# A two-layer hybrid block on one core: the first mixer's latent products in two items and other banks, its filling pieces dealt out anew, its output projection begun two heads sooner

## The chip, the cores and the metric

The kernel runs as one launch on one core of a Trainium2 chip. The metric is the device time of one execution in microseconds (us); lower is better. The engines are named as in the profile: PE (TensorE, matrix products, with PEld for its weight loads), DVE (VectorE), ACT (ScalarE), POOL (GpSimd) and SP (SyncE, which here only issues transfers).

## The reference

Two layers run over 512 tokens of width 1024. Layer 0 mixes tokens with the "even mixer", layer 1 with another one, and a gated, convolved feed-forward network of width 2816 follows each. The change lies almost wholly in the even mixer:

```python
def even_mixer(h, positions, w_in, q_norm, w_uq, kv_norm, w_ukv, w_out):
    proj = h @ w_in
    q, k, v = ...                      # 12 heads of 64, three groups of four
    q, k = rope(q, positions), rope(k, positions)
    for window, dilation in ((128, 1), (512, 4), (2048, 16)):
        out, lse = dilated_window_attention(q[group], k[group], v[group], window, dilation)
    y_a = sum over the groups of softmax(lse) * out        # four heads of 64
    qm = rmsnorm(c_q, q_norm) @ w_uq   # 12 heads of 64 + 32, from a latent of 256
    kv = rmsnorm(c_kv, kv_norm) @ w_ukv  # 12 heads of 64 + 64, from a latent of 128
    y_b = causal_softmax_attention(q_full, k_full, v_m, 96 ** -0.5)
    return concatenate([y_a, y_b]) @ w_out    # 1024 -> 1024, added to x by the caller
```

## The kernel before

All values are fp32. A product is made of three matmuls of rounded halves (`mm3`: high by high, high by low, low by high). So each weight block is loaded as `wraw`, its high half `whi` is made by ACT (L220) and its low half `wlo` by DVE or POOL (L222). Two buffers of each kind serve all weights (`wchunk`). Activations are split in the same way into `xh` and `xl`.

The even mixer lays its attention out as 16 head steps: heads 0 to 5 and 8 to 13 are the latent ("MLA") heads in pairs `pr` 0 to 5, and heads 6, 7, 14 and 15 are the windowed ("dsw") heads, where one step serves one head of all three groups. A head's scores go to the PSUM banks `s`; DVE adds the mask and takes the extremum (L580), ACT takes the exponent and scales (L582, L584). PE then turns the weights around in the banks `t`, ACT and DVE split them into `pth` (L601, L954) and `ptl` (L602, L955), and PE applies them to the values in the banks `o`. While head k is turned and applied in `units`, the scores of head k+1 are made. There are two banks each of `s`, `t`, `o` and `proj`.

PE's order is fixed by the program (`InOrder`); the order on the other engines is chosen by a scheduler when the kernel is built. Between the steps of a head, PE gets *pieces* from a `Stream` of items: one piece is one product of three 512-column matmuls. `st.fill(n)` takes n pieces, `st.until(name)` takes as many as finish an item, and an item that is held (`holds`, with the head that frees it) blocks the stream. The items are: projections of q, k (`d{p}{g}{s}`) and v for the dsw heads, eight pieces each; the latent products `m{pr}` for a pair of MLA heads, six pieces; `y`, which splits the finished heads' outputs; and `o0` to `o7`, the output projection, one for each 128 rows of x. `F_M`, `F_D0` and `F_D1` say how many pieces a head takes after each score, after each turn and at its end, `F_V` how many around a value transpose.

Latent products use the banks `proj`: in `run_mla`, v (tile `vt`, L761), k (`knp`, L766), then two queries (`rt`, L775). The output projection runs over seven of the eight tiles of y; the eighth, from the last dsw pair, is added by `run_tail` after head 15, one product and one `residual` (L367) for each of the eight tiles of x. Then the feed-forward network's `norm` makes `xh` (L331) and `xl` (L332) of x.

Of the kernel before, what the change touches and what calls it, by code (L numbers as in the profile page):

```python
# [18 lines left out]
P = 128  # L19
# [32 lines left out]
F_V = 1, 2  # L52
F_M, F_D0, F_D1 = (1, 1, 2), (2, 1.5, 3), (2, 2, 4)
# [131 lines left out]
class Builder:  # L185
# [169 lines left out]
    def run_tail(self, src, kt, y, banks=("proj",)):  # L355

        def run(w):
            for m in range(KT):
                ps = self.psum(banks[m % len(banks)])
                self.gemm(ps, w, m * P, P, 0, {kt: y[kt][0]}, {kt: y[kt][1]}, [kt])  # L360
                self.residual(m, ps)
                yield

        return f"t{kt}", lambda: self.wchunk(src, D), run

# [143 lines left out]
    def ffn(self, pool, g, cw, cb, wg, wu, wd, tiles=KT):  # L509

        nc = self.nc
        pre = [self.wchunk(w[0], D) for w in (wg, wu)]
# [132 lines left out]
    def even_mixer(self, pool):  # L645
# [109 lines left out]

        def run_mla(pr):
            def run(w):
                vps = self.psum("proj")
                self.gemm(vps, w, 640, P, 0, klh, kll, [0])
                vt = pool.tile([P, T], F32, tag="tmp", name=self.nm("vt"), bufs=TMP)  # L760
                nc.vector.tensor_tensor(vt, vps, kr, op=ALU.mult)  # L761
                yield
                kps = self.psum("proj")
                self.gemm(kps, w, 512, P, 0, klh, kll, [0])
                knp = pool.tile([P, T], F32, tag="knp", name=self.nm("knp"), bufs=1)
                nc.vector.tensor_tensor(knp, kps, kr, op=ALU.mult)  # L766
                yield
                qs = []
                for e in range(2):
                    qps = self.psum("proj")  # L770
                    for i in range(2):
                        self.gemm(qps, w, e * P + i * 256, P, 256, qlh, qll, [i], i == 0, i == 1)
                        yield
                    t = pool.tile([P, T], F32, tag="tmp", name=self.nm("rt"), bufs=TMP)
                    nc.vector.tensor_tensor(t, qps, qt[e], op=ALU.mult)  # L775
                    qs.append(self.split(t, pool, **QK))
                    if e == 0:
                        v = self.token_split(pool, vt, "v", 3)
                yp = pool.tile([P, T], F32, tag="yp", name=self.nm("yp"), bufs=6)
                mla[pr] = qs, v, yp, knp  # L780

            return f"m{pr}", lambda: self.wchunk(a["wm0"][pr], 768), run

        def run_out(m):
            def run(w):
                yh, yl = {k: y[k][0] for k in range(7)}, {k: y[k][1] for k in range(7)}
                for ps in self.proj_pieces(w, yh, yl, range(7)):
                    yield
                self.residual(m, ps)

            return f"o{m}", lambda: self.wchunk(a["wo0"][m], 896), run

        def run_y():
            def run(w):
                for i in range(6):
# [7 lines left out]
        def y_split(kt, yp):  # L803
# [7 lines left out]
               for p in range(2)]  # L811
        m = [run_mla(pr) for pr in range(6)]
        st = Stream(dsw[0][:3] + m[:1] + dsw[0][3:4] + m[1:2] + dsw[0][4:6] + m[2:3] + dsw[0][6:]
                    + dsw[1][:2] + m[3:4] + dsw[1][2:4] + m[4:5] + dsw[1][4:6] + m[5:] + dsw[1][6:]
                    + [run_y()] + [run_out(m) for m in range(KT)])

        holds = {"d022": 5, "m3": 7, "d110": 7, "d122": 13, "y": 14}
# [47 lines left out]
        def mla_head(pr, e):  # L865
            hd = Head()
            hd.fill_s, hd.fill_u, hd.fill_g = F_M
# [31 lines left out]
            def finish():  # L899
                self.head_out(pool, hd.o, mla[pr][2], e)  # L900

# [826 lines left out]
```

## Time and profile before

| what | value |
|---|---|
| median of 3 runs | 1448.83 us (1447.15 to 1449.09) |
| the profiled execution's own time | 1443.72 us |
| its span, first to last instruction | 1441.7 us |
| mean granted TensorE clock in it | 0.993 |
| PE busy | 1380.4 us (96%) |
| DVE busy | 872.8 us (61%) |
| ACT busy | 696.3 us (48%) |

The even mixer takes the first 336 us of the span. An engine's row in a timeline may end with the idle time ahead of it and, behind an arrow, the instruction that ended it. A matmul's record lasts longer than its share of PE, since the next one starts before it ends; starts that follow each other give that share.

### The profile page before, as it was taken

To read this page: it belongs to the slowest core of one execution; us is meant where nothing else is said; L and a number is where in the kernel's file an instruction comes from. 1 tells how busy PE (TensorE), PEld (TensorE's weight loads), DVE (VectorE), ACT (ScalarE), POOL (GpSimd) and SP (SyncE) were. 2 spreads that over 40 slices of the span, in tenths; PEclk is the share of its full clock that TensorE was granted. 3 is DMA by queue.
4 is the path that set the end of the run, shared out by engine and by line. 5 is a ranking of instruction groups with operands and counts; after the bars stand their busy time and mean duration, and the time that the engine had idled before them with its cause. 6 is when DMAs were issued, how large, how long until landed. Compare 5 with 4: busy or idle time off the path is not lost.

```text
span 1441.7 us, 17940 instructions
## 1 busy us (share of the span) xinstructions
PE 1380.4 (96%) x6796; PEld 1139.2 (79%) x6796; DVE 872.8 (61%) x1393; ACT 696.3 (48%) x1151; POOL 413.1 (29%) x249
## 2 busy tenths in 40 slices
PE   7899899999999999999998998999999999999997
PEld 5677777787888888888887777787888888888886
DVE  7978778747555555212578997789555555552124
ACT  5578668735433333222366565787344333333322
POOL 2100000003655555444200000222025555554440
PEclk9999999999999999999999999999999999999998
DMA  5422122122233232333222111111222232333333
GB/s 169 121 58 61 56 70 68 42 68 88 88 103 98 93 102 88 104 96 93 90 84 68 59 45 61 47 57 48 75 92 95 100 102 88 103 99 93 97 95 99
DMA packets 40262, 121.19 MB, mean 84 GB/s; under 512 B 5233, under 2 KB 8305, under 8 KB 40177
## 3 DMA queue, kind: packets, MB, share of 16 engines
q1 hardware_dynamic: 38160, 117.92, 26.2%
q10 hardware_dynamic: 2016, 2.14, 0.5%
q8 instruction: 53, 0.87, 0.3%
q14 instruction: 33, 0.26, 0.1%
HBM read 114.80 MB, written 2.10 MB: 81 GB/s over the span
## 4 chain that ended last, share of the span: by engine, by line
PE 77%; DVE 14%; ACT 4%; issue 3%; DMA 1%; POOL 0%; SPq 0%; DVEq 0%; ACTq 0%; POOLq 0%
PE proj L113 48%; PE o L113 19%; PE z L113 5%; PE s L113 2%; DVE wlo L222 2%; PE t L116 2%; PE t L113 1%; ACT whi L220 1%; DVE cv L1153 1%; ACT s L582 1%; ACT s L584 1%; DVE xl L332 0%; DVE ptl L602 0%; DVE mh L266 0%; DVE xs L1393 0%
## 5 line engine op out<-in xcount | busy, mean ns | idle before, releaser
L222 POOL TENSOR_TENSOR wlo<-wraw,whi 128x1024 fp32r<-128x1024 f32 (+1 forms) x135 | 315.2, 2336 | 574.0 <-ACT whi L220 574.0
L220 ACT ACTIVATE whi<-wraw 128x1024 fp32r<-128x1024 f32 (+3 forms) x219 | 222.1, 1015 | 354.9 <-PE proj L113 322.7
L113 PE MATMUL proj<-xh,whi 128*128 128x512 f32 x844 | 341.8, 405 | 8.5 <-ACT xh L331 6.4
L113 PE MATMUL proj<-xh,wlo 128*128 128x512 f32 x844 | 332.7, 394 | 1.3 <-DVE wlo L388 1.1
L113 PE MATMUL proj<-xl,whi 128*128 128x512 f32 x844 | 332.9, 394 | 1.1 <-DVE xl L332 1.1
L113 PE MATMUL proj<-act,whi 128*128 128x512 f32 (+1 forms) x748 | 219.3, 377 | 0.0
L113 PEld LDWEIGHTS proj<-xh,whi 128*128 128x128 f32 x844 | 160.2, 190 | 40.8 <-ACT xh L331 8.6
L113 PEld LDWEIGHTS proj<-xh,wlo 128*128 128x128 f32 x844 | 160.0, 190 | 37.1 <-DVE wlo L388 1.5
L113 PEld LDWEIGHTS proj<-xl,whi 128*128 128x128 f32 x844 | 160.4, 190 | 31.0 <-DVE xl L332 3.0
L113 PEld LDWEIGHTS proj<-act,whi 128*128 128x128 f32 x748 | 137.7, 188 | 25.7
L113 PE MATMUL o<-xh,wlo 128*128 128x512 f32 x368 | 143.5, 390 | 0.0
L113 PE MATMUL o<-xh,whi 128*128 128x512 f32 x368 | 143.5, 390 | 0.0
L113 PE MATMUL o<-xl,whi 128*128 128x512 f32 x368 | 143.3, 389 | 0.0
L113 PE MATMUL proj<-act,wlo 128*128 128x512 f32 (+1 forms) x374 | 140.9, 377 | 0.0
L367 DVE TENSOR_TENSOR x<-x,proj 128x512 f32<-128x512 f32 x31 | 21.2, 685 | 171.6 <-PE proj L113 171.5
L525 DVE SCALAR_TENSOR_TENSOR cv<-gt,cols,cv 128x511 f32<-128x511 f32 x44 | 94.3, 2147 | 35.9 <-ACT cv L524 35.9
L222 DVE TENSOR_TENSOR wlo<-wraw,whi 128x1024 fp32r<-128x1024 f32 (+3 forms) x84 | 95.7, 1139 | 28.8 <-ACT whi L220 27.9
L528 ACT ACTIVATE sl<-cv 128x512 f32<-128x512 f32 x44 | 27.8, 631 | 127.3 <-DVE cv L526 127.3
L534 DVE TENSOR_TENSOR up<-sl,o 128x512 f32<-128x512 f32 x44 | 30.3, 688 | 91.9 <-POOL sl L529 91.9
L529 POOL TENSOR_TENSOR sl<-sl,rsr 128x512 f32<-128x512 f32 x44 | 57.8, 1313 | 94.3 <-ACT sl L528 94.3
L266 DVE TENSOR_TENSOR act<-up,act 128x512 fp32r<-128x512 f32 x44 | 63.2, 1437 | 29.3 <-ACT act L265 29.3
L113 PEld LDWEIGHTS proj<-act,wlo 128*128 128x128 f32 x374 | 70.4, 188 | 12.9
(305 smaller groups left out, 2126.7 us busy)
## 6 DMA issues: line engine op xcount, KB each, us to landing
wraw<-in_g SPq DMA_DIRECT2D x44, 512.0 KB, 3.4
wraw<-in_u SPq DMA_DIRECT2D x44, 512.0 KB, 3.3
wraw<-in_d SPq DMA_DIRECT2D x32, 448.0 KB, 3.3
wraw<-in_wqk SPq DMA_DIRECT2D x20, 512.0 KB, 3.6
wraw<-in_d SPq DMA_DIRECT2D x17, 512.0 KB, 3.5
wraw<-in_wx SPq DMA_DIRECT2D x12, 512.0 KB, 3.3
wraw<-in_wv SPq DMA_DIRECT2D x10, 512.0 KB, 3.5
wraw<-in_wz SPq DMA_DIRECT2D x8, 512.0 KB, 3.3
```

Of the source, the lines that this page charges most:

```text
L113: return self._put(self.b.nc.tensor.matmul(*args, **kw))
L116: return self._put(self.b.nc.tensor.transpose(*args))
L220: nc.scalar.activation(hi[:, :n], raw[:, :n], AF.Copy)
L222: (eng or self.lo).tensor_tensor(lo[:, :n], raw[:, :n], hi[:, :n].bitcast(F32), op=ALU.subtract)
L266: nc.vector.tensor_tensor(lo, src, hi.bitcast(F32), op=ALU.subtract)
L367: self.nc.vector.tensor_tensor(self.x[m], self.x[m], ps, op=ALU.add)
L525: nc.vector.scalar_tensor_tensor(c[:, 1:], gt[:, : T - 1], col_(1), c[:, 1:], op0=ALU.mult, op1=ALU.add)
L528: nc.scalar.activation(s, c, AF.Silu)
L529: nc.gpsimd.tensor_tensor(s, s, r, op=ALU.mult)
L534: nc.vector.tensor_tensor(u, s, pu, op=ALU.mult)
L582: nc.scalar.activation(t, t, AF.Exp, bias=nmx, scale=-1.0, accum_out=l)
L584: nc.scalar.activation(t, t, AF.Copy, scale=rl)
```

## The change

**Latent products.** An item `m` now has four pieces: v in a bank `s`, the first half of query 0 in `proj`, k in a bank `s`, the second half of query 0. A new item `n` without weights of its own has the two pieces of query 1, with the transpose of v between them. `hd.needs` has `n{pr}` done by the start of the pair's first head.

**Pieces.** Four pieces are taken ahead of the very first scores and one after them (before: none extra ahead, four after). MLA heads of the first three pairs take one piece at their end instead of two, the first dsw pair takes 1 instead of 1.5 after a turn, and the holds change. The stacking of the first dsw operand is called one head sooner.

**Output projection.** `y` is freed at head 12 instead of 14. It then covers six tiles of y (0 to 4 and 6, weights 768 wide instead of 896). Tiles 5 and 7 come in a tail of two items: eight accumulators in all eight banks, 16 pieces, each accumulator read once.

**Feed-forward.** In both networks the low halves of the first two weight blocks are made by DVE instead of POOL.

The built programs have the same 6,579 PE instructions; DVE has 5 more, POOL 4 fewer, ACT and SP one more each. Counted in PE's order, the stream's 244 pieces stand like this, from a head's first turn to the next head's:

| | to head 0 | 0 | 1 | 2 | 3 | 4 | 5 | 6 | 7 | 8 | 9 | 10 | 11 | 12 | 13 | 14 | 15 and tail |
|---|---|---|---|---|---|---|---|---|---|---|---|---|---|---|---|---|---|
| before | 38 | 10 | 10 | 10 | 10 | 5 | 16 | 11 | 19 | 10 | 10 | 10 | 10 | 4 | 8 | 22 | 41 |
| now | 37 | 9 | 9 | 9 | 9 | 10 | 13 | 16 | 16 | 12 | 10 | 10 | 10 | 11 | 14 | 21 | 28 |

On PE in head 0, at the latent products of the next pair, there stood before (the number behind a name is a buffer's; `lh`, `ll` are the latents' halves, `kh` and `qk` keys and queries, `pth` and `ptl` turned weights):

```order
L113 MATMUL s_152_752<-kh1_572,qk_119_636 128x512
L113 MATMUL proj_155_762<-lh_62_365,whi_122_644 128x512
L113 MATMUL proj_155_762<-ll_63_366,whi_122_644 128x512
L113 MATMUL proj_155_762<-lh_62_365,wlo_123_646 128x512
L113 MATMUL o_137_713<-pth_139_718,v_115_623 128x128
L113 MATMUL o_137_713<-ptl_140_719,v_115_623 128x128
L116 MATMUL t_157_770<-ident_108,s2_133_683 128x128
L116 MATMUL t_157_770<-ident_108,s3_130_670 128x128
L116 MATMUL t_157_770<-ident_108,s4_127_657 128x128
L113 MATMUL proj_160_778<-lh_58_357,whi_122_644 128x512
```

and now:

```order
L113 MATMUL s_144_729<-kh1_572,qk_120_639 128x512
L113 MATMUL s_151_751<-lh_62_365,whi_122_644 128x512
L113 MATMUL s_151_751<-ll_63_366,whi_122_644 128x512
L113 MATMUL s_151_751<-lh_62_365,wlo_123_646 128x512
L113 MATMUL o_137_710<-pth_139_715,v_117_630 128x128
L113 MATMUL o_137_710<-ptl_140_716,v_117_630 128x128
L116 MATMUL t_153_759<-ident_108,s2_133_689 128x128
L116 MATMUL t_153_759<-ident_108,s3_130_676 128x128
L116 MATMUL t_153_759<-ident_108,s4_127_663 128x128
L113 MATMUL proj_156_767<-lh_58_357,whi_122_644 128x512
L113 MATMUL s_157_771<-kh1_572,qk_119_638 128x384
```

Before, k (`proj_155`) and query 0 (`proj_160`) follow v (`proj_150`) in the two `proj` banks, so query 0 needs v's bank back. Now v stands in `s_151`, query 0 in a `proj` bank of its own, and the next to share a bank with v is k.

On DVE at the same place, before (`wlo` is the low half of a weight block, `rot` a rotated projection, ISA the mask-and-extremum instruction):

```order
L222 TENSOR_TENSOR wlo_149_744<-wraw_147_740,whi_148_742 128x1024
L761 TENSOR_TENSOR vt_151_750<-proj_150_746,rsr_94_519 128x512
L732 TENSOR_TENSOR rot_146_731<-proj_124_648,cos_274 128x512
L602 TENSOR_TENSOR ptl_140_719<-t_138_716,pth_139_718 128x128
L580 ISA s4_154_757,st_153_756<-s_152_752,masks_371 128x512
```

and now:

```order
L569 ISA s4_146_734,st_145_733<-s_144_729,masks_371 128x512
L569 ISA st_145_733 128x1
L764 TENSOR_TENSOR vt_152_755<-s_151_751,rsr_94_519 128x512
L222 TENSOR_TENSOR wlo_173_821<-wraw_171_817,whi_172_819 128x1024
L721 TENSOR_TENSOR rot_149_741<-proj_124_648,cos_274 128x512
```

The scheduler has moved `vt` ahead of the weights' low half, and the mask of the score ahead of both.

On DVE at the end of the mixer, before (`x0` to `x7` are x's tiles with the bank that is added, `xl` and `sq` belong to the feed-forward's norm; the low halves of its first weights stand on POOL):

```order
L367 TENSOR_TENSOR x2_90<-x2_90,s_780_3357 128x512
L332 SCALAR_TENSOR_TENSOR xl_793_3408<-x0_83,cols_70,xh_792_3407 128x512
L367 TENSOR_TENSOR x3_92<-x3_92,proj_781_3362 128x512
L367 TENSOR_TENSOR x4_94<-x4_94,s_782_3367 128x512
L332 SCALAR_TENSOR_TENSOR xl_795_3412<-x1_88,cols_70,xh_794_3411 128x512
```

and now:

```order
L356 TENSOR_TENSOR x4_94<-x4_94,proj_785_3349 128x512
L222 TENSOR_TENSOR wlo_791_3405<-wraw_789_3401,whi_790_3403 128x1024
L356 TENSOR_TENSOR x5_99<-x5_99,o_786_3357 128x512
L332 SCALAR_TENSOR_TENSOR xl_802_3426<-x3_92,cols_70,xh_801_3425 128x512
L356 TENSOR_TENSOR x6_101<-x6_101,proj_787_3365 128x512
L348 TENSOR_TENSOR sq_811_3445<-sq_811_3445,sq_814_3453 128x512
```

The additions to x now have the norm's first steps between them, and the low half of the network's first weights with them.

The diff, cut to its core:

```diff
-F_V = 1, 2
-F_M, F_D0, F_D1 = (1, 1, 2), (2, 1.5, 3), (2, 2, 4)
+F_V = 1, 1
+F_M0, F_M, F_D0, F_D1 = (1, 1, 1), (1, 1, 2), (2, 1, 3), (2, 2, 4)
...
-        pre = [self.wchunk(w[0], D) for w in (wg, wu)]
+        pre = [self.wchunk(w[0], D, nc.vector) for w in (wg, wu)]
...
+        def mla_query(pr, k, w, between):
+            qps = self.psum("proj")
+            for i in range(2):
+                self.gemm(qps, w, k * P + i * 256, P, 256, qlh, qll, [i], i == 0, i == 1)
+                yield
+                if i == 0:
+                    yield from between()
+            t = pool.tile([P, T], F32, tag="tmp", name=self.nm("rt"), bufs=TMP)
+            nc.vector.tensor_tensor(t, qps, qt[k], op=ALU.mult)
+            mla[pr][0].append(self.split(t, pool, **QK))
...
-                vps = self.psum("proj")
+                vps = self.psum("s")
...
+                def keys():
+                    kps = self.psum("s")
...
+                yield from mla_query(pr, 0, w, keys)
...
+        def run_mla2(pr):
+            def run(_):
+                def values():
+                    mla[pr][1] = self.token_split(pool, mla[pr][1], "v", 3)
...
+                yield from mla_query(pr, 1, mla[pr].pop(), values)
+            return f"n{pr}", lambda: None, run
...
+        def tail():
+            banks = ("s", "t", "s", "t", "proj", "o", "proj", "o")
...
+            first = [(5, m) for m in range(4)]
+            rest = [p for m in range(4) for p in ((7, m), (5, m + 4))] + [(7, m) for m in range(4, 8)]
...
-        holds = {"d022": 5, "m3": 7, "d110": 7, "d122": 13, "y": 14}
+        holds = {"d022": 4, "m3": 6, "n3": 8, "d122": 11, "y": 12}
...
+                if pr == 5 and e:
+                    st.until("y")
+                    y_split(5, mla[5][2])
...
+        st.fill(4)
         for i in (3, 2, 1, 0):
             st.fill(1)
             heads[0].score(i)
-        st.fill(4)
+        st.fill(1)
...
-        st.add([self.run_tail(a["wo0b"], 7, y, ("s", "proj"))])
+        st.add(tail())
```

More of the change, by code (lines that the diff above doesn't have):

```diff
@@ L353, in x_rstd @@
         return self.token_rstd([self.x_squares(pool)], [D], "x", self.small, ["rsr"])[0]
[L355 to L364, printed above, removed]
     def residual(self, m, ps):
@@ L762, in run @@
                 yield
[L763 to L778, printed above, removed]
@@ L787, in run, with product, pieces @@
-                for ps in self.proj_pieces(w, yh, yl, range(7)):
+                kts = (0, 1, 2, 3, 4, 6)
+                yh, yl = {k: y[k][0] for k in kts}, {k: y[k][1] for k in kts}
+                for ps in self.proj_pieces(w, yh, yl, kts):
                     yield
                 self.residual(m, ps)
-            return f"o{m}", lambda: self.wchunk(a["wo0"][m], 896), run
+            return f"o{m}", lambda: self.wchunk(a["wo0"][m], 768), run
+        def tail():
+            banks = ("s", "t", "s", "t", "proj", "o", "proj", "o")
+            ps, ws = {}, []
+            def product(kt, m):
+                if kt == 5:
+                    ps[m] = self.psum(banks[m])
+                self.gemm(ps[m], ws[kt == 7], m * P, P, 0, {kt: y[kt][0]}, {kt: y[kt][1]}, [kt], kt == 5, kt == 7)
+                if kt == 7:
+                    self.residual(m, ps[m])
+            def run(which):
+                def pieces(w):
+                    ws.append(w)
+                    for p in which:
+                        product(*p)
+                        yield
+                return pieces
+            first = [(5, m) for m in range(4)]
+            rest = [p for m in range(4) for p in ((7, m), (5, m + 4))] + [(7, m) for m in range(4, 8)]
+            return [(f"t{i}", lambda i=i: self.wchunk(a["wo0b"][i], D), run(p)) for i, p in enumerate((first, rest))]
@@ L793, in run_y @@
         def run_y():
             def run(w):
-                for i in range(6):
+                for i in range(5):
                     y_split(i, mla[i][2])
@@ L866, in mla_head @@
             hd = Head()
-            hd.fill_s, hd.fill_u, hd.fill_g = F_M
+            hd.fill_s, hd.fill_u, hd.fill_g = F_M if pr > 2 else F_M0
+            hd.needs = f"n{pr}"
             def prepare():
@@ L905, in even_mixer, with stack @@
         qk, vs, yps = {}, {}, {}
+        def stack(p, s):
+            st.until(f"d{p}0{s}")
+            qk[p, 0, s] = self.stacked(raws[p, 0, s], s, lambda: pool.tile([P, T], F32R, name=self.nm("qk"), **QK))
         def dsw_head(p, e):
@@ L1017, in even_mixer @@
             heads[0].score(i)
-        st.fill(4)
+        st.fill(1)
         for k, hd in enumerate(heads):
             nxt = heads[k + 1] if k + 1 < len(heads) else None
+            st.held -= {name for name in holds if holds[name] <= k}
+            if hd.needs:
+                st.until(hd.needs)
             units = hd.units()
             n = len(units)
-            st.held -= {name for name in holds if holds[name] <= k}
+            if k in (4, 11):
+                stack(k // 11, 0)
             if nxt:
```

31 lines of the change are left out of this document (19 added, 12 removed).

## The prediction

> **What bounds the kernel now.** First the page's busy times: PE is busy for 96% of the span, no other engine for more than 61%.
>
> ```profile
> span 1441.7 us, 17940 instructions
> PE 1380.4 (96%) x6796; PEld 1139.2 (79%) x6796; DVE 872.8 (61%) x1393; ACT 696.3 (48%) x1151; POOL 413.1 (29%) x249
> ```
>
> The change leaves PE's instructions as they are, so it can win or lose only what PE idles. Second, the view of busy times by stretch, cut at the heads' first turns (columns: stretch, its length, busy time and count of PE, PEld, DVE, ACT, POOL, granted clock, share of the DMA engines, GB/s):
>
> ```profile
> 55.00:77.80 22.80, 18.11 (x73) 13.21 (x72) 17.69 (x34) 12.69 (x24) 0.00 (x0) 0.93 0.26 75
> 77.80:128.40 50.60, 47.28 (x249) 39.00 (x248) 44.89 (x103) 40.83 (x90) 0.00 (x0) 1.00 0.23 66
> 128.40:159.00 30.60, 28.68 (x203) 23.12 (x202) 19.39 (x46) 21.12 (x47) 0.00 (x0) 1.00 0.16 49
> 159.00:198.90 39.90, 35.07 (x251) 29.16 (x250) 28.12 (x56) 23.80 (x45) 0.00 (x0) 1.00 0.25 69
> 198.90:250.20 51.30, 47.44 (x249) 39.29 (x248) 46.10 (x106) 41.49 (x93) 0.00 (x0) 1.00 0.21 64
> 250.20:299.00 48.80, 45.25 (x347) 36.22 (x346) 31.70 (x72) 33.55 (x69) 0.00 (x0) 1.00 0.16 48
> 299.00:350.00 51.00, 48.49 (x238) 39.98 (x237) 31.79 (x42) 21.19 (x30) 8.95 (x4) 1.00 0.23 73
> 350.00:1441.70 1091.70, 1064.17 (x4984) 882.71 (x4982) 607.99 (x857) 472.07 (x713) 392.00 (x231) 0.99 0.27 86
> ```
>
> Length less PE busy is PE's idle time: 4.69 us ahead of head 0, 3.32 in heads 0 to 3, 1.92 in 4 and 5, 4.83 in 6 and 7, 3.86 in 8 to 11, 3.55 in 12 to 14, 2.51 in head 15 and the way into the feed-forward network: 24.7 us in all. That is the ceiling of a gain here. DVE tells the stages apart: it is busy for 89% of heads 0 to 3 and 90% of heads 8 to 11, but for 63 to 70% of heads 4 to 7 and 65% of 12 to 14.
>
> Third, who ended PE's waits between 55 and 300 us (total, times, longest):
>
> ```profile
> PE proj L113 <- DVE vt L761: 6.9, 6, 1.6
> PE o L113 <- DVE ptl L602: 4.7, 5, 1.2
> PE s L113 <- DVE qk L266: 3.2, 2, 2.8
> PE t L116 <- DVE ptl L955: 2.7, 1, 2.7
> PE t L116 <- DVE v L630: 2.6, 4, 1.1
> ```
>
> Nearly all are DVE's. The single rows I use:
>
> ```profile
> 61.50 0.50 PE L113 MATMUL proj<-lh,whi 128*128 128x512 f32 x1 [1.30 <-DVE vt L761]
> 66.28 0.50 PE L113 MATMUL s<-kh,qk 128*128 128x512 f32 x1 [0.55 <-ACT qk L265]
> 69.85 0.50 PE L113 MATMUL s<-kh,qk 128*128 128x512 f32 x1 [2.84 <-DVE qk L266]
> 135.62 0.50 PE L113 MATMUL o<-pth,v 128*128 128x512 f32 x1 [0.52 <-ACT pth L601]
> 137.33 0.50 PE L113 MATMUL o<-ptl,v 128*128 128x512 f32 x1 [1.21 <-DVE ptl L602]
> 160.02 0.66 PE L116 MATMUL t<-ident,s 128*128 128x128 f32 x4 [0.58 <-DVE v L630]
> 174.72 0.50 PE L113 MATMUL proj<-lh,whi 128*128 128x512 f32 x1 [1.59 <-DVE vt L761]
> 181.19 0.66 PE L116 MATMUL t<-ident,s 128*128 128x128 f32 x4 [2.66 <-DVE ptl L955]
> 258.01 0.50 PE L113 MATMUL o<-ptl,v 128*128 128x512 f32 x1 [1.11 <-DVE ptl L602]
> 261.79 0.44 PE L116 MATMUL t<-ident,s 128*128 128x128 f32 x2 [0.67 <-DVE v L630]
> 271.18 0.44 PE L113 MATMUL o<-ptl,v 128*128 128x384 f32 x1 [0.60 <-DVE ptl L602]
> 277.01 0.74 PE L116 MATMUL t<-ident,s 128*128 128x128 f32 x4 [1.13 <-DVE v L630]
> ```
>
> **The change part by part.** The price of a piece comes from the first and the last of 18 matmuls in a row without a wait:
>
> ```profile
> 321.80 0.39 PE L113 MATMUL proj<-xh,whi 128*128 128x512 f32 x1
> ...
> 325.65 0.39 PE L113 MATMUL proj<-xh,wlo 128*128 128x512 f32 x1
> ```
>
> 3.85 us over 17 steps is 0.2265 us, and a piece of three is 0.68 us.
>
> *Ahead of head 0.* The first score waits for DVE's work, and over the last wait the view by stretch has DVE without a gap:
>
> ```profile
> 66.85:69.85 3.00, 0.16 (x1) 0.00 (x1) 3.00 (x6) 1.47 (x2) 0.00 (x0) 1.00 0.00 0
> 70.50:73.85 3.35, 3.35 (x11) 2.87 (x10) 1.41 (x6) 2.25 (x5) 0.00 (x0) 0.50 0.39 147
> ```
>
> DVE's list up to there holds the same instructions as before, so the score stays near 69.85. But three pieces stand ahead of it now instead of one: two run inside the wait, 1.36 us won. The waits at 61.50 and 66.28 fold into the later one (DVE is as late as it was), so they count for nothing here. Bounds: 0, if DVE comes later by as much, and 3.1 with the clock below. Taken: -1.36.
>
> The second row shows the clock at 0.50 for 3.35 us after the wait of 2.84, while the wait of 2.66 at 181 us left it at 1.00. Three waits (1.30, 0.55, 2.84: 4.69) less two pieces leave about 3.3 us in one block, longer than the 2.84 that was enough; so I keep the slow stretch in both kernels. [...]
>
> *Heads 0 to 3*, nine pieces each instead of ten. Four pieces are 2.72 us less for PE, but DVE sets the pace. An eight-piece projection costs DVE its weights' low half (1.14 us, the mean of the row below) and three rotations of about 0.7, some 0.4 us a piece: four pieces relieve DVE of 1.6 us only. PE's idle time grows by the rest, 1.1, and the stacking called a head sooner adds to a full stage, some 0.5. Against that, two of the `vt` waits lie here, and they shorten: `vt` stood behind a low half,
>
> ```profile
> 78.84 1.23 DVE L222 TENSOR_TENSOR wlo<-wraw,whi 128x1024 fp32r<-128x1024 f32 x1 [2.23 <-ACT whi L220]
> 79.98 0.68 DVE L761 TENSOR_TENSOR vt<-proj,rsr 128x512 f32<-128x512 f32 x1
> ```
>
> and now goes ahead of it, so the bank is free 1.2 us sooner; I credit half a microsecond, since the low half then delays the score's mask. Bounds: -1.5 (both waits gone, DVE keeps up) and +2.72 (the four pieces become idle time). Taken: +1.0, DVE's share being the nearest row.
>
> *Heads 4 and 5.* Head 4 had five pieces and waited 0.52 and 1.21 at its end; it has ten now, 3.4 us more cover, and DVE has room. Of 1.92 idle, -1.4. Bounds: -1.9 and 0.
>
> *Heads 6 and 7.* Before, all six pieces of `m3` ran in a burst ahead of head 7 and head 8's first score: the waits of 1.59 and 2.66 stand in it, since DVE got `vt`, `knp` and both `rt` at once. Now four pieces fill head 6 and two fill head 7. Of the 4.25 I take 3.0; bounds -4.25 and -1.3 (the burst's work is still DVE's).
>
> *Heads 8 to 11*, two pieces more and DVE 90% busy: three `vt` or bank waits of 3.86 idle shorten as in heads 0 to 3, -1.0. Bounds: -2.4 and +1.0.
>
> *Heads 12 to 14* get 46 pieces instead of 34, since `y` is free two heads sooner; heads 12 and 13 had four and eight, and waited 1.11, 0.67, 0.60, 1.13. Output pieces are cheap for DVE: a low half and an addition for six. -2.2; bounds -3.5 and -1.0 (the splits of y come into DVE's list here). The end pays for it: 28 pieces are left instead of 41, 8.8 us, which is no gain of its own but where the earlier pieces come from.
>
> *The tail.* Before, eight additions fell due at once, and the network began with three waits:
>
> ```profile
> 333.18 0.47 PE L113 MATMUL proj<-xh,whi 128*128 128x512 f32 x1 [1.58 <-DVE x L367]
> 336.86 0.50 PE L113 MATMUL proj<-xl,whi 128*128 128x512 f32 x1 [0.69 <-DVE xl L332]
> 348.32 0.49 PE L113 MATMUL proj<-xh,wlo 128*128 128x512 f32 x1 [0.24 <-POOL wlo L222]
> ```
>
> Now x's first tiles fall due 11 pieces (7.5 us) ahead of PE's end, so DVE starts earlier, but the two low halves join its list. Their price and what it gives back:
>
> ```profile
> L222 DVE TENSOR_TENSOR wlo<-wraw,whi 128x1024 fp32r<-128x1024 f32 (+3 forms) x84 | 95.7, 1139 | 28.8 <-ACT whi L220 27.9
> 331.10 0.74 DVE L332 SCALAR_TENSOR_TENSOR xl<-x,cols,xh 128x512 fp32r<-128x512 f32 x1
> 333.83 2.42 POOL L222 TENSOR_TENSOR wlo<-wraw,whi 128x1024 fp32r<-128x1024 f32 x1 [4.41 <-ACT whi L220]
> 334.82 1.98 DVE L332 SCALAR_TENSOR_TENSOR xl<-x,cols,xh 128x512 fp32r<-128x512 f32 x1
> ```
>
> An `xl` took 1.98 beside POOL's low half, 0.74 without: 2 x 1.23 more, at least 1.24 less. Of 2.51 idle, -1.0; bounds -2.0 and +0.5. The second network's start has no wait of PE's in the trace; its two low halves are hidden by the last projection, 0, at worst +1.0 if the last `xl` goes behind the second of them.
>
> The narrower weights, the extra tail block and the moved transfers go at nothing: SP's order keeps each swap behind the same weights, and DMA is busy for about a quarter of these stages.
>
> Sum: -1.36 + 1.0 - 1.4 - 3.0 - 1.0 - 2.2 - 1.0 = -9.0 us. The profiled execution took 1443.7 us, 2.0 more than its span, and would take 1434.7. The runs' median, 1448.8, lies 5.1 above it; the same step from it gives **1440** (0.62% less). A change under 0.2% (2.9 us) could not be told from none here.
>
> **The rivals.** *DVE is the bound, and the pieces only move the idle time:* for it speak the 89 and 90%. Then heads 0 to 3 lose 2.7, 8 to 11 lose 1.0, and the rest gives half or less (0.7, 0.7, 1.5, 1.0, 0.5): -0.7, so 1448. Against it: the longest waits lie where DVE is busy for 70% or less. Chance 0.20.
>
> *Slower: the scores' banks.* A latent product now holds an `s` bank until DVE has multiplied it, k waits for v's, and the score after it for k's or for a mask that stands behind a low half. Before, query 0 came some 1.9 us of PE work after v (a score and k at 0.68 each, five narrow matmuls) and still waited 6.9 / 6 = 1.15 on average, so `vt` lagged by 3.05; k now comes after about 1.8 (query 0 and a 384-wide score in the place of the other two). If the lag stays, each of the five later pairs waits 1.25 at k and, as an estimate, as much again at the score: 12.5, less 9.0 is +3.5, 1452. It decides from 1.8 us a pair on. Against it: `vt` left the place behind the low half. Chance 0.13.
>
> [...] Chance 0.10.
>
> *Nearly every wait goes:* the far bounds from head 4 on (1.9, 4.25, 2.4, 3.5, 2.0) with the 1.36, and heads 0 to 3 at +0.5: -14.9, 1434. Chance 0.15.
>
> **How the numbers follow.** The forecast has 0.42, its own range 1436 to 1445. The range from 1434 to 1450 leaves out the slower rival and what lies beyond the last. Faster: 0.41 + 0.10 + 0.15 + a little of the first rival, 0.70; same 0.16; slower 0.14.
>
> **What would show it.** Right: the first score still near 70 us with PE free of waits until some 65; no `vt` wait on `proj`; none above 1 us in heads 4 and 12 to 14; idle time in heads 0 to 3 at 4 us or more; additions to x from five pieces into the tail. Wrong: waits of `s` for `vt`, `knp` or the mask, over 1 us a pair; new waits for `wlo` right behind an `n` item, whose two pieces are a short lead for the next weights; a second slow stretch of the clock.

## The result: 0.7% slower, where a gain of 0.6% was forecast

The changed kernel took 1455.54 us (median of 10 runs, 1453.92 to 1463.11), the kernel before 1447.88 us beside it (10 runs, 1445.47 to 1449.23). The ratio is 1.0066, with a 95% interval of 1.0055 to 1.0078. Forecast were 1440 us and a range up to 1450: the sign is wrong. Three of the ten runs took 1462.6 to 1463.1 us at a mean granted clock of 0.981, the other seven had 0.987 to 0.990 and the kernel before, in the rounds of the experiments below, 0.989 to 0.993, so the ratio, which counts every run, is larger than that of the two medians (1.0053). The clock belongs to the explanation, as will be seen.

The page of the changed kernel; its profiled execution took 1453.92 us:

```profile
span 1452.2 us, 17955 instructions
PE 1387.0 (96%) x6796; PEld 1143.1 (79%) x6796; DVE 873.7 (60%) x1398; ACT 696.1 (48%) x1152; POOL 403.1 (28%) x245
```

The view by stretch, cut at the same first turns as before (stretch, length, busy time of PE, PEld, DVE, ACT, POOL, granted clock, DMA share, GB/s):

```profile
55.00:78.00 23.00, 19.66 (x78) 14.36 (x77) 19.50 (x36) 11.80 (x22) 0.00 (x0) 0.93 0.31 83
78.00:128.70 50.70, 45.62 (x238) 38.24 (x237) 43.03 (x101) 39.28 (x90) 0.00 (x0) 0.97 0.23 66
128.70:161.40 32.70, 29.33 (x205) 23.51 (x204) 20.10 (x46) 22.92 (x49) 0.00 (x0) 1.00 0.15 45
161.40:202.20 40.80, 37.83 (x261) 30.82 (x259) 28.18 (x54) 24.32 (x47) 0.00 (x0) 1.00 0.20 55
202.20:262.90 60.70, 50.94 (x256) 41.42 (x255) 48.54 (x109) 42.69 (x95) 0.00 (x0) 0.97 0.23 68
262.90:318.10 55.20, 52.60 (x383) 42.93 (x382) 35.36 (x76) 34.21 (x71) 0.00 (x0) 1.00 0.18 53
318.10:350.00 31.90, 30.89 (x152) 25.01 (x151) 24.37 (x34) 18.25 (x27) 0.00 (x0) 1.00 0.24 83
350.00:1452.20 1102.20, 1074.47 (x5032) 890.96 (x5030) 611.96 (x864) 473.93 (x715) 391.31 (x230) 0.99 0.27 85
```

PE's idle time is now 3.34, 5.08, 3.37, 2.97, 9.76, 2.60 and 1.01 us, 28.1 in all against 24.7, so 3.4 more. The stretch of heads 8 to 11 alone went from 3.86 to 9.76. And the clock was 0.97 in two stretches where it had been 1.00: the trace has seven slow stretches of 3.41 us at 0.50 between 40 and 900 us, three before. Four more cost, by estimate from these figures (half of 3.41), up to 1.7 us each, 6.8; with the 3.4 that makes 10.2 of the 10.5 us between the two spans. PE's busy time says the same: it is 6.6 us longer for the same 6796 matmuls. Two of the four (at 117.9 and 223.7 us) lie in the changed part. The other two (46.2, 889.3) lie in code that the change does not touch, and the trace of the kernel before has 1.00 there; some 2.7 us of the 10.5 (1.6 and 1.1 in the table of the terms) are theirs, and not the change's. In the timed runs the clock's median went from 0.990 (82 runs of the kernel before, beside the experiments) to 0.9875, by estimate some 3.6 us of the 7.7.

Who ended PE's waits (the view of waits, 55 to 318 us: total, times, longest), and single rows of PE's timeline, those that matter:

```profile
PE t L116 <- DVE v L619: 7.6, 6, 2.6
PE s L113 <- DVE qk L266: 5.3, 3, 2.8
PE o L113 <- DVE ptl L591: 5.1, 6, 1.8
PE s L113 <- ACT qk L265: 4.6, 2, 2.4
```

```profile
72.06 0.50 PE L113 MATMUL s<-kh,qk 128*128 128x512 f32 x1 [2.79 <-DVE qk L266]
115.74 0.50 PE L113 MATMUL s<-kh,qk 128*128 128x512 f32 x1 [2.20 <-ACT qk L265]
132.57 0.33 PE L113 MATMUL o<-pth,v 128*128 128x128 f32 x1 [1.31 <-ACT pth L590]
205.08 0.41 PE L116 MATMUL t<-ident,s 128*128 128x128 f32 x2 [2.64 <-DVE v L619]
217.65 0.39 PE L113 MATMUL proj<-lh,wlo 128*128 128x512 f32 x1
221.46 0.50 PE L113 MATMUL s<-kh,qk 128*128 128x512 f32 x1 [2.40 <-ACT qk L265]
223.84 0.80 PE L113 MATMUL s<-kh,qk 128*128 128x512 f32 x1 [1.55 <-DVE qk L266]
278.05 0.44 PE L116 MATMUL t<-ident,s 128*128 128x128 f32 x2 [1.83 <-DVE v L619]
```

The 6.9 us of `proj` waiting for `vt` are gone, as forecast. In their place scores wait for the query halves `qk` and turns for `v`. Worst are heads 3 and 9: the last matmul of pair 4's query 0 starts at 217.65, and the score that needs that query, about a microsecond of PE's work later, at 221.46. The timelines of DVE and ACT in between:

```profile
219.94 0.67 DVE L754 TENSOR_TENSOR rt<-proj,qt 128x512 f32<-128x512 f32 x1
...
223.09 0.69 DVE L266 TENSOR_TENSOR qk<-rt,qk 128x512 fp32r<-128x512 f32 x1
```

```profile
220.78 0.63 ACT L265 ACTIVATE qk<-rt 128x512 fp32r<-128x512 f32 x1
```

DVE takes up the query 2 us after it stands in its bank, and the low half 2.5 us after that, behind `ptl`, `kl` and `sw`. Before, the other query's two pieces and more lay between a query and its first score. The pair's item now ends at the very edge of head 9, because one more projection (`d120`, eight pieces) stands ahead of it in the stream; in head 3 it is the four pieces taken from heads 0 to 3. The stream's new order is part of the change, though the diff ahead of the prediction leaves its lines out (`dsw[1]` are the second pair's projections in order, so `dsw[1][4]` is `d120`):

```diff
-                    + dsw[1][:2] + m[3:4] + dsw[1][2:4] + m[4:5] + dsw[1][4:6] + m[5:] + dsw[1][6:]
...
+                    + dsw[1][:2] + m[3][:1] + dsw[1][2:4] + m[3][1:] + dsw[1][4:5] + m[4] + dsw[1][5:6] + m[5]
```

### The profile page after: what moved, and what is told of

Its sections match the earlier page's. It is cut to its first block, busy times and chain, and to the rows that moved or that the text cites. A ratio compares the mean times of both kernels' runs of the same rounds, so it can differ in the third digit from the quotient of the medians.

```text
span 1452.2 us, 17955 instructions
## 1 busy us (share of the span) xinstructions
PE 1387.0 (96%) x6796; PEld 1143.1 (79%) x6796; DVE 873.7 (60%) x1398; ACT 696.1 (48%) x1152; POOL 403.1 (28%) x245
## 4 chain that ended last, share of the span: by engine, by line
PE 77%; DVE 13%; ACT 5%; issue 2%; DMA 1%; POOL 0%; SPq 0%; DVEq 0%; ACTq 0%; POOLq 0%
PE proj L113 47%; PE o L113 20%; PE z L113 5%; PE s L113 3%; DVE wlo L222 2%; PE t L113 2%; PE t L116 1%; ACT whi L220 1%; DVE cv L1200 1%; ACT s L571 1%; DVE s L569 0%; DVE ptl L591 0%; DVE kl L910 0%; DMA x<-in_x 0%; DVE ab L1608 0%
## 5 line engine op out<-in xcount | busy, mean ns | idle before, releaser
L222 POOL TENSOR_TENSOR wlo<-wraw,whi 128x1024 fp32r<-128x1024 f32 (+1 forms) x131 | 305.6, 2333 | 592.9 <-ACT whi L220 536.6
L222 DVE TENSOR_TENSOR wlo<-wraw,whi 128x1024 fp32r<-128x1024 f32 (+3 forms) x89 | 100.7, 1132 | 28.7 <-ACT whi L220 27.8
L113 PEld LDWEIGHTS o<-xh,wlo 128*128 128x128 f32 x372 | 69.8, 188 | 15.3 <-DVE wlo L222 0.8
L113 PEld LDWEIGHTS o<-xh,whi 128*128 128x128 f32 x372 | 69.9, 188 | 15.1 <-DVE x L356 0.7
```

The source lines that it names most:

```text
L113: return self._put(self.b.nc.tensor.matmul(*args, **kw))
L222: (eng or self.lo).tensor_tensor(lo[:, :n], raw[:, :n], hi[:, :n].bitcast(F32), op=ALU.subtract)
```

## The experiments

Ratios are to the kernel before, run on the same chip, with 95% intervals; five rounds each. The diffs are cut to the lines that matter. The recorded texts give some waits 0.16 us longer than the rows of the timelines do (4.17 for 4.01, 3.8 for 3.62, 1.13 for 0.97).

**One part at a time on the kernel before.** The banks alone:

```diff
-                vps = self.psum("proj")
+                vps = self.psum("s")
...
-                kps = self.psum("proj")
+                kps = self.psum("s")
```

> The kernel before with one edit: v and k of the latent products go to the banks s instead of proj. Theory 1: the six waits of proj for vt (6.9 us in the profile before) go, nothing takes their place in full, 1444 to 1447. Rival (the scores' banks, my recorded one): waits of s for vt, knp or the mask take their place, 1.25 us or more a pair, 1449 to 1452.

Measured: 1449.38 us, ratio 1.0002 (0.9993 to 1.0011). Neither: no loss, no gain. The waits of `proj` for `vt` went. Of `s` for `vt` there are three now, 2.7 us in all and 1.1 at most, which is the rival's wait at a smaller size; and in the burst ahead of head 8 the others came back as one wait. Before, that place had 1.59 at 174.72 and 2.66 at 181.19; with the banks changed PE's timeline has

```profile
183.47 1.12 PE L116 MATMUL t<-ident,s 128*128 128x128 f32 x4 [4.06 <-DVE ptl L955]
```

and the two matmuls of 512 columns behind it take 0.78 and 0.63 us, as the first two do in the changed kernel's stretch at 0.50 (118.46, 119.04); behind the 2.66 before they took 0.47 and 0.39.

The pieces alone:

```diff
-F_V = 1, 2
-F_M, F_D0, F_D1 = (1, 1, 2), (2, 1.5, 3), (2, 2, 4)
+F_V = 1, 1
+F_M0, F_M, F_D0, F_D1 = (1, 1, 1), (1, 1, 2), (2, 1, 3), (2, 2, 4)
...
-        holds = {"d022": 5, "m3": 7, "d110": 7, "d122": 13, "y": 14}
+        holds = {"d022": 4, "m3": 6, "d122": 13, "y": 14}
...
+        st.fill(4)
         for i in (3, 2, 1, 0):
...
-        st.fill(4)
+        st.fill(1)
```

> The kernel before with the pieces alone: four pieces ahead of the first score, the fills of one piece at a head's end in the first three pairs, the first dsw pair's fills, the holds d022 at 4 and m3 at 6, the stacking a head sooner. Six-piece latent items in proj banks, the output projection as before. Theory 1: the pieces do no harm, by the recorded terms -1.4 +1.0 -1.4 and some -2 in heads 6 and 7, 1444 to 1447. Rival (the fewer pieces in heads 0 to 3 cost what they leave): 1449 or more, with more idle time in heads 0 to 3 than the 3.3 us before.

Measured: 1451.92 us, ratio 1.0022 (1.0013 to 1.0032), without one run of 3531 us. The rival holds in time, and in part in place: PE idles 4.61 us in heads 0 to 3 (3.32 before), and 8.78 in heads 4 to 7 (6.75 before), with matmuls of 512 columns at 0.63 us and more behind the waits at 128.04 and 159.11, where 0.40 is usual in this profile. The start gained. Single rows of PE's timeline, and the stretch of heads 8 to 11 (columns as above):

```profile
69.59 0.50 PE L113 MATMUL s<-kh,qk 128*128 128x512 f32 x1 [0.97 <-DVE qk L266]
128.04 0.33 PE L113 MATMUL o<-ptl,v 128*128 128x128 f32 x1 [1.68 <-DVE ptl L602]
159.11 0.93 PE L116 MATMUL t<-ident,s 128*128 128x128 f32 x4 [1.94 <-DVE v L630]
```

```profile
201.20:252.50 51.30, 47.43 (x249) 39.24 (x248) 46.10 (x106) 41.47 (x93) 0.00 (x0) 1.00 0.22 64
```

The wait ahead of the first score is 0.97 where it was 2.84, and no slow stretch follows: the matmuls of 512 columns from 69.94 to 72.69 take 0.39 or 0.40 us. Heads 8 to 11 idle 3.87 us, as before (3.86): here the stream's order is the old one, so the fewer pieces of heads 0 to 3 do not by themselves make their loss in the changed kernel.

The output projection alone (`y` at head 12, six tiles, the tail of eight banks):

```diff
-        holds = {"d022": 5, "m3": 7, "d110": 7, "d122": 13, "y": 14}
+        holds = {"d022": 5, "m3": 7, "d110": 7, "d122": 11, "y": 12}
...
-        st.add([self.run_tail(a["wo0b"], 7, y, ("s", "proj"))])
+        st.add(tail())
```

> The kernel before with the output projection alone: y free at head 12, six tiles of y ahead, two in the tail of eight banks. Theory 1: not touched by the loss; by the recorded terms -2.2 and -1.0, about 1445. Rival (the additions and y's splits only move the wait): 1448, within 0.2% of before. If it is slower than 1450, the tail has a share in the loss.

Measured: 1445.14 us, ratio 0.9979 (0.9968 to 0.9990). The forecast's two terms here, -2.2 and -1.0, agree in their sum with what the runs show (-3.0, from -1.4 to -4.6); the run does not tell them apart, and the network's low halves on DVE, which the second term counts too, are not in it.

The latent items alone, then with v's transpose put ahead of query 1:

```diff
+            hd.needs = f"n{pr}"
...
-        m = [run_mla(pr) for pr in range(6)]
+        m = [[run_mla(pr), run_mla2(pr)] for pr in range(6)]
```

> The kernel before with the latent items alone: items m and n, the new order v, half of query 0, k, other half, half of query 1, transpose of v, other half; v and k in the banks s; fills, holds and output projection as before. Since a head's preparation now waits for m and not for all six pieces, two pieces fewer stand ahead of head 0. Theory (transpose): turns waiting for v at heads 3 and 8 or 11, 3 to 5 us slower than before, 1451 to 1453. Rival (only the pieces dealt anew cost time, the item's form is free): 1447 to 1449.

> The same with v's transpose ahead of query 1's first half. Theory (transpose): the loss of the run before it goes, 1446 to 1449. Rival (query 0 begun before k, or the split, costs by itself): as slow as that run.

Measured: 1450.24 us, ratio 1.0011 (1.0003 to 1.0020), and 1452.51 us, 1.0027 (1.0019 to 1.0036). Inconclusive: the first is a small loss, with the waits where the theory put them (4.6 us for `v` at 120, 4.0 at 244); the second did not mend it, as the rival there had said. There the waits for `v` fell to half (12.3 to 6.5 us in all), but in head 7 a wait of 4.33 us of the transpose itself took their place. The four parts do not add up to the change: -0.21, +0.22 and +0.11% (the last has the banks in it) make +0.12%, and the change cost 0.66%. None of them has the stream's new order, in which pair 4 comes behind `d120`, nor the network's low halves on DVE.

**One edit at a time on the changed kernel.** First the split undone, the rest kept:

```diff
-                    + dsw[1][:2] + m[3][:1] + dsw[1][2:4] + m[3][1:] + dsw[1][4:5] + m[4] + dsw[1][5:6] + m[5]
+                    + dsw[1][:2] + m[3] + dsw[1][2:4] + dsw[1][4:5] + m[4] + dsw[1][5:6] + m[5]
...
-        holds = {"d022": 4, "m3": 6, "n3": 8, "d122": 11, "y": 12}
+        holds = {"d022": 4, "m3": 6, "d122": 11, "y": 12}
...
             def prepare():
-                st.until(f"m{pr}")
+                st.until(f"n{pr}")
```

> The changed kernel with the latent item in one piece again: a head's preparation waits for item n instead of m, so all six pieces stand ahead of the next head's scores, and m3 and n3 are neighbours; banks, fills, tail are those of the change. Theory 1 (the split puts query 0 only a piece or two ahead of the score that needs it, heads 3 and 9 lose 4.3 and 7.0 us there, and each wait halves the clock): no wait of a score for qk over 1 us between 110 and 230 us, no slow clock at 118 and 224 us, and 9 to 11 us less than the changed kernel, about 1445. Rival (the banks s for v and k make the loss): still 1453 or more. Rival (the fills make it): 1452 or more, with the loss still in heads 3 and 9.

Measured: 1455.7 us, ratio 1.0051 (1.0036 to 1.0067). My first theory, that the split as such was the cause, fell. The waits for `qk` went and longer ones for `v` stood in the same two heads (single rows of PE's timeline):

```profile
116.27 0.66 PE L116 MATMUL t<-ident,s 128*128 128x128 f32 x2 [4.72 <-DVE v L619]
222.37 0.66 PE L116 MATMUL t<-ident,s 128*128 128x128 f32 x2 [3.62 <-DVE v L619]
```

What is late differs, the place does not. So the next runs moved the items' places.

```diff
-                    + dsw[1][:2] + m[3][:1] + dsw[1][2:4] + m[3][1:] + dsw[1][4:5] + m[4] + dsw[1][5:6] + m[5]
+                    + dsw[1][:2] + m[3][:1] + dsw[1][2:4] + m[3][1:] + m[4] + dsw[1][4:6] + m[5]
```

> The changed kernel with one edit in the stream's order: the latent products of pair 4 stand eight pieces earlier, ahead of the projection d111 and not behind it, so that both items are done in head 8 and none is left for head 9. The run before fell the first theory (the split as such): with the items joined the scores' waits for qk went, and waits of the turns for v of 4.7 and 3.8 us stood in the same heads 3 and 9. New theory, lead: a latent item that ends at the edge of its deadline makes PE wait for whatever DVE's full list brings last, query or value, and halves the clock; what put it there is the pieces dealt anew, not the split. It expects no wait over 1 us at the first score for head 10 or at its first turn (4.0 and 1.8 us now), 5 to 7 us less than the changed kernel's 1455.5: about 1449. Split theory: unchanged, 1455.

Measured: 1452.32 us, ratio 1.0034 (1.0022 to 1.0047), and the waits of 2.40 and 1.55 are gone; the largest in heads 9 to 10 are now 0.49 and 0.58, and the granted clock is 1.00 over heads 8 to 11. (The recorded text calls the projection `d111`; it is `d120`.) The stretch of heads 8 to 11:

```profile
201.60:255.30 53.70, 47.87 (x250) 38.83 (x248) 47.65 (x108) 41.77 (x92) 0.00 (x0) 1.00 0.25 69
```

It took 60.70 in the changed kernel, with two pieces more (1.4 us): PE idles 5.83 us in it and not 9.76, and the clock is 1.00 and not 0.97. This is the one edit that by itself stands clear of the changed kernel's interval. The time gained is less than the 5 to 7 us expected: 0.32% by the ratios, 0.18% by the medians.

```diff
-            hd.fill_s, hd.fill_u, hd.fill_g = F_M if pr > 2 else F_M0
+            hd.fill_s, hd.fill_u, hd.fill_g = F_M if pr != 2 else F_M0
```

> The changed kernel with one number other: the heads 0 to 3 take two pieces at their end again instead of one, so that pair 2's latent items are done four pieces sooner (all in head 2). Four pieces fewer are left for head 7. Lead: the waits at 115.7 and 117.5 us (2.2 and 0.9) and the slow clock at 118 go, 3 to 4.5 us less, about 1451.5. Rival of the record (DVE is the bound of heads 0 to 3, pieces there do not matter): 1455, the wait moved to heads 0 to 3 or to head 7.

Measured: 1454.12 us, ratio 1.0045 (1.0032 to 1.0058): a smaller gain than expected, and its interval touches the changed kernel's. The waits for `qk` in head 3 went, and a wait of 4.01 us for `v` came instead.

```diff
-F_V = 1, 1
+F_V = 1, 2
```

> The changed kernel with one number other: two pieces again, not one, behind the transpose of a windowed head's values. Theory: the changed kernel's waits of a turn for v at 145.2, 278.1 and 296.2 us (1.51, 1.83, 0.76) come from the one piece that is missing there, and the run with the pieces alone lost its 3 us by them; they shrink to the 0.4 to 1.1 of before, 2 to 2.5 us less, about 1453. Rival (v is late whatever the pieces do, DVE's list decides): unchanged, 1455.

Measured: 1455.04 us, ratio 1.0062 (1.0045 to 1.0078). A miss: the waits did shrink (1.51 to 0.82, 1.83 to 1.14), but the pieces that cover them were taken from head 7, and the wait at 203 us grew to 3.06, with matmuls of 512 columns at 0.62 and 0.63 us from 203.62 on (0.39 and 0.40 after the wait at 144.60).

All three edits, with one piece fewer after a score in the first windowed pair:

> The three edits together (pair 4's latent products earlier, two pieces at the end of heads 0 to 3, two behind the value transposes), and the first windowed pair's heads take 1 instead of 2 after a score so that head 7 keeps 13 pieces. If lead and the missing piece are the whole loss: 1455.5 less 6, 4 and 2.3 is 1443, below the kernel before (1448) and at or under the kernel with the output projection alone (1445). If the split or the banks carry a loss of their own: 1447 or more.

Measured: 1447.65 us, ratio 0.9999 (0.9989 to 1.0008). The loss is won back, 0.67% by the ratios and 0.50% by the medians; the three edits alone gave 0.32, 0.21 and 0.04, or 0.18, 0.06 and nothing. The fourth edit, the piece fewer, was not run alone. Of the run's two forecasts the second came, 1447 or more, by which the split or the banks carry a loss of their own. The waits that are left longest are for `v` (4.01 and 3.22). Single rows of PE's timeline and then of DVE's (the last row's `v` is the split of the transposed `vt`):

```profile
113.11 0.60 PE L116 MATMUL t<-ident,vt 128*128 128x128 f32 x4
119.22 0.66 PE L116 MATMUL t<-ident,s 128*128 128x128 f32 x2 [4.01 <-DVE v L619]
```

```profile
115.53 0.68 DVE L608 TENSOR_TENSOR yp<-o,yp 64x512 f32<-64x512 f32 x1
116.14 1.07 DVE L726 TENSOR_TENSOR rot<-rot,sw 128x512 f32<-128x512 f32 x1
117.14 0.68 DVE L754 TENSOR_TENSOR rt<-proj,qt 128x512 f32<-128x512 f32 x1
117.74 0.67 DVE L266 TENSOR_TENSOR qk<-rt,qk 128x512 fp32r<-128x512 f32 x1
118.41 0.67 DVE L619 TENSOR_TENSOR v<-t,v 128x512 fp32r<-128x512 f32 x1
```

The transposed values sit in a bank `t` until DVE, which has no gap here, reaches `v`; the second turn of the head needs that bank. The change had put the transpose one piece ahead of the turn. With two:

```diff
-                def values():
-                    mla[pr][1] = self.token_split(pool, mla[pr][1], "v", 3)
...
-                yield from mla_query(pr, 1, mla[pr].pop(), values)
+                mla[pr][1] = self.token_split(pool, mla[pr][1], "v", 3)
+                yield from mla_query(pr, 1, mla[pr].pop(), lambda: ())
```

> The run with the three edits together (1447.65 against 1447.27 before), with one edit more: item n transposes v ahead of query 1's first half, not between its halves, so that two pieces and not one stand between the transpose and the next head's first turn, which needs a t bank. That run's largest waits are turns waiting for v: 4.17 us at 119.2 and 3.38 at 204.6, the first followed by slow matmuls. Theory (transpose): the new place of v's transpose is the part of the loss that is left; the two waits shrink to under 1.5 us, 4 to 6 us less, about 1442. Rival (DVE's list is full there, v is late by its place in that list): the waits stay over 3 us or move to the scores' qk, 1446 to 1448.

Measured: 1441.12 us, ratio 0.9963 (0.9949 to 0.9976); 6.5 us from that edit by the medians, 5 by the ratios, where the theory had 4 to 6. The two waits are 1.11 and 1.48 now. PE's timeline with the transpose and the turn, then DVE's:

```profile
109.08 0.62 PE L116 MATMUL t<-ident,vt 128*128 128x128 f32 x4
113.46 0.44 PE L116 MATMUL t<-ident,s 128*128 128x128 f32 x2 [1.11 <-DVE v L619]
```

```profile
112.71 0.69 DVE L619 TENSOR_TENSOR v<-t,v 128x512 fp32r<-128x512 f32 x1
```

The two missing corners, the same edit on the changed kernel as it stands, and the old order within the item:

> The changed kernel with one edit: v's transpose ahead of query 1, item order and pieces as changed. Fourth corner to the changed kernel (1455.5), the three edits (1447.65) and those with this one (1441.1). Lead theory with the transpose as a second cause: in the changed kernel heads 3 and 9 wait for query 0 and not for v, so the edit helps only at 205 us (2.64): 1453 to 1455. If the transpose alone makes the loss: 1449 or less.

> The changed kernel with the latent item in the old form and order (v, k, query 0, transpose of v, query 1, six pieces that a head's preparation waits for), v and k in the banks s; pieces, holds, stream places, output projection, network as changed. It differs from the run with joined items (1455.7) in the order within the item alone. Transpose and lead theory: the turns' waits for v at 116 and 222 us (4.7 and 3.8) shrink to 2 or less, the places of pairs 2 and 4 still cost some, 1447 to 1450. Rival (the pieces dealt anew are the whole loss): 1454 or more.

Measured: 1457.21 us, ratio 1.0047 (1.0030 to 1.0063), and 1454.7 us, ratio 1.0045 (1.0033 to 1.0057). Neither mends the changed kernel. With the items at the edge, the transpose put ahead only waits itself (PE's timeline of the first of the two):

```profile
221.09 1.12 PE L116 MATMUL t<-ident,vt 128*128 128x128 f32 x4 [2.50 <-DVE ptl L591]
```

The old order cut the wait in head 3 from 4.72 to 1.53 but left 3.02 in head 9 and 3.84 in head 7; my 1447 to 1450 was too low, and the rival's 1454 or more came. So in these runs the places come first: the order within the item gave its 6.5 us with the places mended and nothing without.

**What was worth keeping.** The output projection, the early pieces and the network's low halves on DVE, on the kernel before (the output projection's lines are those shown above):

```diff
+        st.fill(4)
         for i in (3, 2, 1, 0):
...
-        st.fill(4)
+        st.fill(1)
...
-        pre = [self.wchunk(w[0], D) for w in (wg, wu)]
+        pre = [self.wchunk(w[0], D, nc.vector) for w in (wg, wu)]
```

> The kernel before with the parts that gained or cost nothing by the runs and the traces: the output projection two heads sooner with its tail (1445.1 alone), the four pieces ahead of the first score instead of behind the last (in the run with the pieces alone the first score waited 1.13 us instead of 2.84, and no slow clock followed), and the network's first low halves on DVE. If these add up: 2 to 3 us under the tail alone, about 1442.5. If the early pieces only move the wait into head 0: 1445.

> The best kernel so far (1438.6) with v and k in the banks s as in the change. The banks alone took 3 us of waits away in the timed runs' clock-corrected time, and a lower clock took it back. If banks are a gain without a longer wait elsewhere: 1436 to 1438. My recorded rival: 1440 or more.

Measured: 1438.63 us, ratio 0.9933 (0.9921 to 0.9946), the best of all, 9.6 us under before and 4 under the sum expected, which no run took apart; and with the banks `s` added 1442.52 us, 0.9953 (0.9940 to 0.9966), whose interval just touches the other. So a loss by the banks is likely there and not certain: the mean clock fell from 0.992 to 0.9885 (medians), by estimate worth some 5 us, against 3.9 us in time. In the profiled executions the merged wait in head 7 is there again, 4.06 us against 2.66; the two matmuls of 512 columns behind it take 0.78 and 0.63 us (0.47 and 0.39 in the best, with 3.41 us at 0.51 from 180.37 on), and 3.41 us at 0.50 begin at 264.78. The longest wait for `v` is 1.8 us (1.2 in the best).

## Why the prediction was wrong

Each term again, from the stretches' cuts. A head's lateness is its first turn now less its first turn before, less 0.68 us for each piece more that stands ahead of it (at heads 0, 4, 6, 8, 12, 15: 1, 5, 4 and 1 fewer, then 1 and 13 more; the table of pieces has 3 at head 6, since it counts that head from the transpose of its values and not from its turn): 0.9, 3.7, 5.2, 3.9, 12.0 and 10.3 us.

| term | forecast | measured |
|---|---|---|
| ahead of head 0 | -1.4 | -1.2, and 2.1 that are there ahead of any changed code (1.6 from a slow stretch at 46 us) |
| heads 0 to 3 | +1.0 | +2.8 |
| heads 4, 5 | -1.4 | +1.5 |
| heads 6, 7 | -3.0 | -1.3 |
| heads 8 to 11 | -1.0 | +8.1 |
| heads 12 to 14 | -2.2 | -1.7 |
| tail, to the network's first stage | -1.0 | -0.8 |
| the rest | 0 | +1.1, a slow stretch at 889 us |

*What held.* The first score came at 72.06, 2.1 late with the whole program, so near 70. The two pieces took the place of the earlier waits (idle time 3.34 us against 4.69); the last wait is as long as it was (2.79), and the slow stretch stayed (3.41 us at 0.50, from 73.54 on). The `vt` waits on `proj` went, and idle time in heads 0 to 3 passed 4 us. The output projection and the tail gave nearly what they should, and of the network's three first waits (1.58, 0.69, 0.24) a few of 0.3 and 0.4 are left.

*The step that failed* is the term of heads 8 to 11, "two pieces more and DVE 90% busy: three `vt` or bank waits of 3.86 idle shorten as in heads 0 to 3, -1.0". It took for granted that a latent item overlaps with PE's other work as it did before. It came out at +8.1, nearly half of the 19.5 us between the forecast's -9.0 and the 10.5 by which the profiled span grew. I counted how many pieces a head gets and what each costs DVE. I did not look where, in the stream, the last piece of a pair's latent item stands against the first score that needs it. In the stretch where DVE has the fewest gaps, eight pieces of lead went away from pair 4 and four from pair 2. Moving pair 4 back made that stretch 7.0 us shorter (1.4 of them two pieces that are no longer in it) and the run 0.32% by itself. The bound of +1.0 for that term had no row behind it.

*Two more terms* missed by less, and the same way. In heads 4 and 5 (-1.4, bounds -1.9 and 0) the ten pieces did not take head 4's waits away: 1.31 and 0.55 stand where 0.52 and 1.21 stood; and one piece fewer behind a transpose of values brought a wait of 1.51, which two pieces shrank to 0.82. Heads 6 and 7 gave 1.3 of the 3.0: the burst's two waits went, and one of 1.93 came at 183.39.

*A step that was missing.* I gave no price to the new place of v's transpose, though the change showed it: one piece ahead of the turn instead of two and more. That is 5 to 6.5 us with the places mended. The sum had only `vt`, the product, not its way through a `t` bank.

*The clock* I kept the same in both kernels, and said that the change "can win or lose only what PE idles". That is not so: PE's instructions are the same, and its busy time grew by 6.6 of the 10.5 us. I had listed "a second slow stretch of the clock" as a sign of being wrong, and gave it no chance and no price; by the mean clocks it is, as an estimate, some 3.6 of the 7.7 us.

*The rivals.* The slower one, the scores' banks, has nearly the time (1452) by the wrong mechanism: no wait of `s` for `vt` or `knp` stands in the changed kernel's view of waits. With the banks alone such waits come, 2.7 us in all and not 12.5, and the time is the same (1.0002). The sign of being right "none above 1 us in heads 4 and 12 to 14" failed in 132.57 (1.31) and 278.05 (1.83). That the slow clock goes, for which the chances have 0.10, rested on nothing that a run shows, and it did not come: the stretch at 0.50 behind the first score stayed, after a wait of 2.79. With the pieces alone that wait was 0.97, and no slow stretch followed. That DVE's list sets the pace, the first rival, is true as far as it goes, but it would have given 1448.

*Left open:* why the edit that gave 6.5 us on the mended kernel did not help the kernel before with split items alone, beyond the wait that moved into head 7; why the edits gave more together than one by one, the fourth of them never run alone; and the losses of the pieces alone in heads 4 to 7, which no run took apart.

## What to carry to other kernels

When filling work is dealt out anew, do not only count it: for each producer find its last instruction in the order, the first that needs it, and what the busiest engine has to do in between. An item that ends just in time for PE is late if its result still has to pass DVE, ACT and DVE again while DVE has no gaps (the scores at 221.46 and 223.84 waited 2.40 and 1.55 us). And do not merge waits: 1.59 and 2.66 us apart from each other left the granted clock at 1.00 in the kernel before (159.00 to 198.90), and behind one of 4.06 matmuls took 0.78 and 0.63 us, not 0.47 and 0.39, in both kernels that had it.

## What the runs showed of the hardware

The prediction set a wait of 2.84, with the clock at 0.50 behind it, against one of 2.66 that left it at 1.00. Their length alone does not tell the two apart: a wait of 2.66 us stands in head 7 of the kernel before (at 181.19), where the clock stayed at 1.00, and, just as long, in the best one (at 179.18), where 3.41 us at 0.51 follow. In the traces of the kernel before and of the changed one each slow stretch lasts 3.41 us, but for the one at the end of the program, and within a trace they start whole steps of that length apart (before at 70.47, 770.20 and 807.75, 205 and 11 steps of 3.413). Cut into such steps between 58 and 335 us, these two traces have four steps at full clock that were followed by one at 0.50. They are the four in which PE was busy least: 0.61 us at 67.05 before, and 0.82, 1.22 and 1.47 us at 220.31, 114.50 and 70.12 in the changed kernel. The other 154 were followed by 1.00; the least busy have 1.57, 1.58 and 1.65 us (203.24, 274.92 and 237.38 in the changed kernel). One of these beside a step of the kernel with the banks on the best (step, length, busy times, and the clock in the third column from the end; the second row of each is the next step):

```profile
274.92:278.34 3.42, 1.58 (x12) 1.14 (x11) 3.27 (x6) 1.40 (x3) 0.00 (x0) 1.00 0.01 2
278.34:281.75 3.41, 3.41 (x32) 2.63 (x31) 1.24 (x4) 1.20 (x3) 0.00 (x0) 1.00 0.43 115
```

```profile
261.37:264.78 3.41, 1.57 (x9) 1.03 (x9) 2.66 (x6) 1.24 (x4) 0.00 (x0) 1.00 0.14 34
264.78:268.19 3.41, 3.41 (x25) 2.47 (x24) 1.17 (x4) 0.82 (x3) 0.00 (x0) 0.50 0.21 81
```

PE busy for 1.58 us of the step was followed by 1.00, 1.57 by 0.50; but 1.57 in the changed kernel's step at 203.24 was followed by 1.00, so PE's busy time parts them in the two traces and not beyond, and the ends of matmuls are modelled. As to the wait of 2.66 us in head 7, before, steps counted from the slow stretch at 70.47 cut it in two:

```profile
176.28:179.69 3.41, 2.25 (x14) 1.70 (x12) 3.29 (x6) 2.50 (x5) 0.00 (x0) 1.00 0.00 0
179.69:183.11 3.42, 1.92 (x11) 1.67 (x12) 2.64 (x4) 1.01 (x2) 0.00 (x0) 1.00 0.39 90
183.11:186.52 3.41, 3.41 (x21) 2.96 (x20) 1.19 (x5) 2.02 (x4) 0.00 (x0) 1.00 0.16 64
```

and in the best kernel's profiled execution 2.2 us of it lie in the step ahead of the slow one:

```profile
176.95:180.37 3.42, 1.19 (x8) 1.07 (x9) 2.77 (x4) 1.62 (x4) 0.00 (x0) 1.00 0.24 37
180.37:183.78 3.41, 3.41 (x10) 2.63 (x9) 1.55 (x4) 1.11 (x4) 0.00 (x0) 0.51 0.29 117
```

So the same wait came with 3.41 us at 0.51 and without, by estimate up to 1.7 us (half of 3.41) of difference. That its place in the step decides is my reading of these rows; no run moved the wait alone. Outside that part of the span the order by PE's busy time does not hold: in the changed kernel PE was busy for all of the step at 42.82 and for 1.86 us of the one at 885.91, and both were followed by 0.50; what those have in common was not tried.
